# Attention scores on 64 rows: two softmax maps on the two row halves of the array

## Chip, cores, metric

The kernel runs on one core of one Trainium2 chip. The metric is the time of one execution in microseconds (us), the median of the runs.

## What is computed

A transformer block with one batch of 1024 tokens and 1024 channels, all in float32: a modulated layer norm, one input projection into queries, keys, values, a pooling branch and two gates, differential attention (8 heads, two softmax maps each), a gated sum with the pooled branch, an output projection, a norm, and a gated feed-forward layer with its norm. The part that matters here is the attention:

```python
def diff_attention(q, k, v, lam, slopes, sub_g, lambda_init):
    """q, k: (B,S,H,2,Dh); v: (B,S,H,Dv); lam: scalar. Returns (B,S,H*Dv)."""
    ...
        bias = -slopes[:, None, None] * dist[None]
        s = jnp.einsum('bqhmd,bkhmd->bhmqk', qblk, k,
                       preferred_element_type=jnp.float32) * scale + bias[None, :, None]
        p = jax.nn.softmax(s, axis=-1)
        a = p[:, :, 0] - lam * p[:, :, 1]
        return jnp.einsum('bhqk,bkhe->bqhe', a, v.astype(jnp.float32))
```

Here m counts the two maps, d the 64 channels of a map's queries and keys, and a block is 128 queries.

## The kernel before

Products run in the type float32r. To keep float32's accuracy, most operands x are split into xh (x rounded to float32r) and xl = x - xh, and a product a b is the sum of three: ah bh, ah bl and al bh (`mm3`, lines 98 to 101). Every TensorE instruction is a weight load of up to 128 x 128 and a product that streams up to 512 columns into one PSUM bank.

The program has a prelude (to 128 us: the first norm, the modulation, the pooling branch and the projections of head 0), the attention (some 128 to 860 us), the output projection and second norm, and the two layers of the feed-forward part. In the attention, the loop at line 808 runs over 8 heads and inside it, at line 855, over 8 blocks j of 128 queries. For one block, `scores` (line 619) forms the scores of both maps against all 1024 keys, a PSUM tile of 128 x 1024 for each (`ps_s`, two buffers in all, two banks each); VectorE adds the distance bias, takes the minimum for the softmax and moves the scores to SBUF (line 635); ScalarE takes the exponentials (line 637); VectorE takes the difference of the two maps (line 642). `transposes` (line 645) turns the result by 8 products with the identity, ScalarE and VectorE split it, and `av` (line 655) multiplies it with the values, 24 products of 256 columns for every second block. In a turn of j the scores of block j+1 are issued ahead of the transposes of block j. Beside that, `fill` (lines 814 to 837) spreads the projections of the next head and the gates over the turns: mostly 24 products of 512 columns for each.

A projection leaves the queries of a head as 128 rows x 512 tokens in PSUM, rows 0 to 63 for map 0 and rows 64 to 127 for map 1. Before, queries and keys are stacked. `evac_k` (line 497) puts kh of a map on its own 64 rows of a tile and kl of the same map on the other 64 rows, a tile for each map. `evac_q` (line 485) splits the queries of a map on its 64 rows into qh and ql, and a DMA copies both to the other 64 rows. A product on all 128 rows then gives qh kh + qh kl at once, and a second one ql kh + ql kl. So a map needs two products for each half of the keys (`kh` in the code counts these halves), and a block eight (lines 628 and 630), one map after the other.

Two parts of the program order their instructions by hand (`manual_schedule`): the prelude and what follows the attention. Within the attention a scheduler of the framework orders the instructions of each engine by priority (earlier in the program first) and by when it reckons that operands and buffers are ready; that order is fixed when the kernel is built. Each engine works through its own queue in order.

Of the kernel before, what the change touches and what calls it, by code (L numbers as in the profile page):

```python
# [9 lines left out]
F32 = mybir.dt.float32  # L10
F32R = mybir.dt.float32r
# [7 lines left out]
P = 128  # L19
# [16 lines left out]
def encoder_block_kernel(  # L36
# [22 lines left out]
    def ps_s(nm):  # L59
        return pp.tile([P, 1024], F32, tag="s", bufs=2, name=nm)  # L60
# [100 lines left out]
    # mod columns: GEMV of rows [128 k x 1024] accumulated on DVE, reduced over partitions by PE  # L161
# [40 lines left out]
    batch = [("u", 3, 3072 + 3 * P), ("u", 2, 3072 + 2 * P), ("q", 0, 0)]  # L202
    wb = {}
    with tc.tile_pool(name="pre", bufs=1, reuse_waits="tile") as pre:
# [99 lines left out]
        def batch_mm(g0, n0=0, n1=6, step=1):  # L304
            """The first products with the contraction outermost, as the tiles of h arrive."""
            if not pq:
                pq.extend((ps_g("pbq0"), ps_g("pbq1")))
            for k, (nm, g, _) in [(k, b) for k in (2 * g0, 2 * g0 + 1) for b in batch][n0:n1:step]:
                for hf in range(2):
                    cs = slice(hf * HF, (hf + 1) * HF)  # L310
                    ps = pq[hf] if nm == "q" else pb[nm, g][:, cs]
                    mm3(ps, wb[nm, g][0][:, k, :], wb[nm, g][1][:, k, :],
                        hT_h[:, k, cs], hT_l[:, k, cs], k == 0, k == KT - 1)
# [13 lines left out]
        def distances(i):  # L327
            """Half of the table of -|key - query|."""
            it = pre.tile([P, 960], I32, tag="hf", bufs=2, name="it%d" % i)
            tf = pre.tile([P, 960], F32, tag="hf", bufs=2, name="tf%d" % i)  # L330
            nc.gpsimd.iota(it, pattern=[[-1, 960]], base=896 - 960 * i, channel_multiplier=1)
            nc.gpsimd.tensor_copy(tf, it)
            return tf
# [77 lines left out]
        # lambda  # L411
# [69 lines left out]
    with ExitStack() as ctx2:  # L481
# [3 lines left out]
        def evac_q(h, hf, ps):  # L485
            sc = 2.0 ** (h - 2)
            for m in range(2):
                r = slice(m * DH, (m + 1) * DH)
                o = slice((1 - m) * DH, (2 - m) * DH)
                t = at1.tile([P, 2, HF], F32R, tag="qd%d" % m, bufs=3, name="q%d_%d_%d" % (h, hf, m))  # L490
                nc.scalar.mul(t[r, 0, :], ps[r, :], sc)
                nc.vector.scalar_tensor_tensor(t[r, 1, :], ps[r, :], sc, t[r, 0, :].bitcast(F32),
                                               op0=ALU.mult, op1=ALU.subtract)
                nc.sync.dma_start(t[o].bitcast(F32), t[r].bitcast(F32))
                qd[h, hf, m] = t

        def evac_k(h, hf, ps):
            cs = slice(hf * HF, (hf + 1) * HF)
            for m in range(2):
                if hf == 0:  # L500
                    kd[h, m] = at1.tile([P, S], F32R, tag="kd%d" % m, bufs=2, name="k%d_%d" % (h, m))
                t = kd[h, m]
                r = slice(m * DH, (m + 1) * DH)
                o = slice((1 - m) * DH, (2 - m) * DH)
                nc.scalar.copy(t[r, cs], ps[r, :])
                nc.vector.tensor_tensor(t[o, cs], ps[r, :], t[r, cs].bitcast(F32), op=ALU.subtract)
# [14 lines left out]
        # ---- pooling branch, with the projections of head 0  # L521
# [97 lines left out]
        def scores(h, j, zt):  # L619
            slope = 2.0 ** -(h + 1)  # L620
            hf, jj = divmod(j, 4)
            s = []
            for m in range(2):
                ps = ps_s("s%d_%d_%d" % (h, j, m))
                q = qd[h, hf, m]
                for kh in range(2):
                    cs = slice(kh * HF, (kh + 1) * HF)
                    nc.tensor.matmul(ps[:, cs], q[:, 0, jj * P:(jj + 1) * P], kd[h, m][:, cs],  # L628
                                     start=True, stop=False)
                    nc.tensor.matmul(ps[:, cs], q[:, 1, jj * P:(jj + 1) * P], kd[h, m][:, cs],  # L630
                                     start=False, stop=True)
                t = at.tile([P, S], F32, tag="s%d" % m, bufs=2, name="e%d_%d_%d" % (h, j, m))
                nm = small.tile([P, 1], F32, tag="nm", bufs=6, name="nm%d_%d_%d" % (h, j, m))
                o0 = 896 - P * j
                nc.vector.tensor_tensor_reduce(out=t, in0=ps, in1=table[:, o0:o0 + S], scale=-slope,  # L635
                                               scalar=3.0e38, op0=ALU.add, op1=ALU.min, accum_out=nm)
                nc.scalar.activation(t, t, AF.Exp, bias=nm, scale=-1.0, accum_out=zt[:, m, j:j + 1])  # L637
                s.append(t)
            c1 = small.tile([P, 1], F32, tag="c1", bufs=4, name="c1_%d_%d" % (h, j))
            nc.vector.reciprocal(c1, zt[:, 1, j:j + 1])  # L640
            nc.vector.tensor_scalar(c1, c1, nlam, zt[:, 0, j:j + 1], op0=ALU.mult, op1=ALU.mult)
            nc.vector.scalar_tensor_tensor(s[1], s[1], c1, s[0], op0=ALU.mult, op1=ALU.add)  # L642
            return s[1]
# [69 lines left out]
        # remaining modulation vectors  # L713
# [14 lines left out]
        # output projection; its first tiles run beside the last head  # L728
        ypart = {}

        def wo_scale(k):
            """w_out with its columns scaled by the gate g1, kept in DRAM until the last head."""
# [51 lines left out]
        def early_load(t):  # L784
            pool, tags, n = {0: (at1, ("kd0", "kd1"), 2), 1: (at1, ("qd0", "qd1"), 3), 4: (at1, ("vh", "vl"), 1),
# [171 lines left out]
    def rest_w(f, rawg, rawu, step):  # L957
        """Operands (gate, up columns) of the last five products of pair f: their sums and splits."""
# [183 lines left out]
    # Each pair of column tiles (gate, up) over both token halves is a 2x2 block product  # L1142
    # with seven block products (Winograd's form).
# [5 lines left out]
    def first_out():  # L1149
        """Operands of the first two steps of the second layer."""  # L1150
# [32 lines left out]
    # Token halves, halves of the hidden channels and column halves form 2x2 blocks again;  # L1183
    # the sums of blocks replace blocks that no later product reads.
    mA = big.tile([P, 16, HF], F32, tag="A", name="mA")
    mB = big.tile([P, 16, HF], F32, tag="B", name="mB")
    with tc.tile_pool(name="fo", bufs=1, reuse_waits="tile") as fo:
# [32 lines left out]
        def sums(q, k):  # L1220
            """Blocks, or sums of blocks, of the hidden activations and of the weights for two steps of product q."""
# [45 lines left out]
        def residual(z, c, cs, xr):  # L1267
            """z = alpha * x1 + g2 * c on the columns cs."""
# [3 lines left out]
        def shift(st):  # L1272
            """-mean * rstd, the bias of the norm on ScalarE."""
# [196 lines left out]
```

## Time and profile before

| | us |
|---|---|
| median of 3 runs | 1675.31 |
| lowest and highest run | 1674.59, 1677.12 |
| span of the profiled execution | 1677.4 |
| TensorE products busy in it | 1578.5 (94%) |
| VectorE busy | 1189.5 (71%) |
| ScalarE busy | 709.9 (42%) |
| GpSimd busy | 421.7 (25%) |
| score products, line 628 | 105.3 (256 products) |
| score products, line 630 | 101.5 (256 products) |

The profile is of one execution. Busy time is the union of the recorded instructions of an engine. Products on TensorE overlap (a record runs from the start of a product to its modelled end), so a group's busy time is more than the time for which it keeps the engine from other work; the starts tell that. PE stands for products and PEld for weight loads, DVE is VectorE, ACT ScalarE, POOL GpSimd, SP the engine that issues most DMAs.

### The profile page before, as it was taken

What the parts mean: (1) busy time and instruction counts of PE and PEld (TensorE: products, weight loads), DVE (VectorE), ACT (ScalarE), POOL (GpSimd) and SP (SyncE); (2) the same over time, 40 slices, a digit from 0 to 9 for tenths busy, and PEclk for the clock granted to TensorE, in tenths of its full rate; (3) what the DMA queues carried; (4) which work ended last, traced back from release to release, by engine and by line L of the source; (5) the groups of instructions that cost most, each with busy time, mean ns of one, the idle gap of its engine ahead of it and who ended that gap; (6) DMA issues with size and microseconds to landing.
All of it is one profiled execution on the core that took longest, in us unless ns stands there. A gap on an engine that the chain in (4) does not pass through costs nothing.

```text
span 1677.4 us, 20367 instructions
## 1 busy us (share of the span) xinstructions
PE 1578.5 (94%) x7634; PEld 1308.7 (78%) x7634; DVE 1189.5 (71%) x1664; ACT 709.9 (42%) x1228; POOL 421.7 (25%) x382
## 2 busy tenths in 40 slices
PE   5899999999999999999989979999999999969874
PEld 3787888888888888888878757888888888858653
DVE  7676868685966667675657896555555554898998
ACT  3445545454545545454532444333333334425341
POOL 4300001010102101000142471212111111574793
PEclk8999999999999999999999989999999999989997
DMA  9244334151433323213063513322322228724321
GB/s 332 60 122 145 105 95 132 45 150 64 133 94 101 120 82 119 57 57 101 27 224 131 170 51 100 97 80 78 99 76 86 77 89 290 255 76 150 107 107 63
DMA packets 169333, 190.76 MB, mean 114 GB/s; under 512 B 7185, under 2 KB 125010, under 8 KB 169234
## 3 DMA queue, kind: packets, MB, share of 16 engines
q1 hardware_dynamic: 165392, 176.06, 33.6%
q0 software_dynamic: 3184, 12.32, 2.0%
q8 instruction: 60, 0.98, 0.2%
q10 hardware_dynamic: 658, 1.08, 0.2%
q14 instruction: 39, 0.32, 0.1%
HBM read 144.34 MB, written 36.70 MB: 108 GB/s over the span
## 4 chain that ended last, share of the span: by engine, by line
PE 75%; DVE 14%; issue 4%; DMA 3%; POOL 3%; ACT 1%; SPq 0%; DVEq 0%; POOLq 0%; ACTq 0%
PE fa L99 4%; PE fa L100 4%; PE fa L101 4%; PE fb L99 3%; PE fb L100 3%; PE fb L101 3%; PE at L651 3%; PE s L628 3%; PE s L630 3%; DVE wo L96 2%; PE pp L99 2%; PE pp L100 2%; PE pp L101 2%; PE pv L99 2%; PE pv L100 2%
## 5 line engine op out<-in xcount | busy, mean ns | idle before, releaser
L637 ACT ACTIVATE e<-e,nm 128x1024 f32<-128x1024 f32 x128 | 147.1, 1150 | 111.1 <-DVE nm L635 109.8
L635 DVE CUSTOM_DVE_ANT_0 e<-s,table 128x1024 f32<-128x1024 f32 x128 | 153.1, 1217 | 24.9 <-PE s L630 24.4
L96 DVE TENSOR_TENSOR ol<-ws,oh 128x512 fp32r<-128x512 f32 x88 | 61.0, 695 | 76.4 <-ACT oh L95 76.3
L628 PE MATMUL s<-k,q 128*128 128x512 f32 x256 | 105.3, 411 | 1.2 <-DVE nm L635 1.2
L96 DVE TENSOR_TENSOR al<-at,ah 128x512 fp32r<-128x512 f32 x128 | 83.2, 684 | 31.9 <-ACT ah L95 31.4
L979 POOL TENSOR_TENSOR ws<-rg,ru 128x512 f32<-128x512 f32 x22 | 45.7, 2075 | 228.1 <-DVE ol L96 217.2
L630 PE MATMUL s<-k,q 128*128 128x512 f32 x256 | 101.5, 397 | 0.0
L95 ACT CAST oh<-ws 128x512 fp32r<-128x512 f32 x88 | 53.9, 616 | 104.4 <-POOL ws L979 66.7
L642 DVE SCALAR_TENSOR_TENSOR e<-e,c,e 128x1024 f32<-128x1024 f32 x64 | 87.4, 1365 | 1.9
L100 PE MATMUL oa<-wo,moh 128*128 128x512 f32 x176 | 73.0, 415 | 15.3 <-DVE wo L96 15.3
L95 ACT CAST ah<-at 128x512 fp32r<-128x512 f32 x128 | 70.0, 596 | 25.1 <-PE at L651 25.1
L99 PE MATMUL oa<-wo,moh 128*128 128x512 f32 x176 | 71.6, 407 | 3.3 <-ACT wo L95 3.3
L651 PE MATMUL at<-ident,e 128*128 128x128 f32 x512 | 68.9, 275 | 6.0 <-DVE e L642 3.2
L99 PE MATMUL av<-ah,vh 128*128 128x256 f32 x256 | 73.9, 289 | 0.3 <-ACT ah L95 0.2
L99 PE MATMUL fa<-oA,oh 128*128 128x512 f32 x176 | 69.8, 397 | 2.9 <-ACT oh L95 2.7
L101 PE MATMUL av<-ah,vl 128*128 128x256 f32 x256 | 72.6, 284 | 0.0
L100 PE MATMUL av<-al,vh 128*128 128x256 f32 x256 | 72.5, 283 | 0.0
L101 PE MATMUL oa<-wo,mol 128*128 128x512 f32 x176 | 71.9, 408 | 0.0
L101 PE MATMUL fa<-oA,ol 128*128 128x512 f32 x176 | 69.7, 396 | 1.1 <-DVE ol L96 1.0
L100 PE MATMUL fa<-oA,oh 128*128 128x512 f32 x176 | 69.6, 396 | 0.5 <-DVE oA L1051 0.5
L681 POOL TENSOR_TENSOR rm_1v<-rm_1s,rm_1v 128x4 f32<-128x4 f32 x8 | 5.0, 624 | 251.8 <-ACT rm_1s L672 251.8
L651 PEld LDWEIGHTS at<-ident,e 128*128 128x128 f32 x512 | 58.7, 144 | 11.7 <-DVE e L642 3.6
(562 smaller groups left out, 4812.3 us busy)
## 6 DMA issues: line engine op xcount, KB each, us to landing
ada<-in_w_ada_dram SPq DMA_DIRECT2D x32, 512.0 KB, 3.8
rg<-in_w_ffn_in_dram SPq DMA_DIRECT2D x26, 512.0 KB, 3.9
w<-in_w_ffn_out_dram SPq DMA_DIRECT2D x24, 512.0 KB, 3.9
ru<-in_w_ffn_in_dram SPq DMA_DIRECT2D x22, 512.0 KB, 3.8
midD<-th SPq DMA_DIRECT2D x42, 256.0 KB, 2.1
q<-q SPq DMA_DIRECT2D x32, 256.0 KB, 2.9
mt<-mixD SPq DMA_DIRECT2D x12, 448.0 KB, 6.4
x<-in_x_dram SPq DMA_DIRECT2D x8, 512.0 KB, 6.3
```

The costliest lines, as they stand in the source:

```text
L95: nc.scalar.copy(hi, src)
L96: (eng or nc.vector).tensor_tensor(lo, src, hi.bitcast(F32), op=ALU.subtract)
L99: nc.tensor.matmul(ps, lh, rh, start=start, stop=False, skip_group_check=skip)
L100: nc.tensor.matmul(ps, lh, rl, start=False, stop=False, skip_group_check=skip)
L101: nc.tensor.matmul(ps, ll, rh, start=False, stop=stop, skip_group_check=skip)
L628: nc.tensor.matmul(ps[:, cs], q[:, 0, jj * P:(jj + 1) * P], kd[h, m][:, cs], start=True, stop=False)
L630: nc.tensor.matmul(ps[:, cs], q[:, 1, jj * P:(jj + 1) * P], kd[h, m][:, cs], start=False, stop=True)
L635: nc.vector.tensor_tensor_reduce(out=t, in0=ps, in1=table[:, o0:o0 + S], scale=-slope, scalar=3.0e38, op0=ALU.add, op1=ALU.min, accum_out=nm)
L637: nc.scalar.activation(t, t, AF.Exp, bias=nm, scale=-1.0, accum_out=zt[:, m, j:j + 1])
L642: nc.vector.scalar_tensor_tensor(s[1], s[1], c1, s[0], op0=ALU.mult, op1=ALU.add)
L651: nc.tensor.matmul(pt[:, i, :], a[:, kt * P:(kt + 1) * P], ident, start=True, stop=True, is_transpose=True)
L979: pol(sa, r11, r21, op=ALU.subtract)
```

## The change

`evac_q` no longer makes a tile for each map and no DMA copies halves: one tile holds qh and ql of both maps on 128 rows, each map on the 64 rows on which the projection left it. `evac_k` likewise splits both maps at once into a tile of kh and one of kl. `scores` then issues, for each half of the keys, qh kh, qh kl and ql kh for each map, each product on 64 rows, in turns between map 0 (rows 0 to 63) and map 1 (rows 64 to 127): twelve products for a block. Both PSUM tiles are asked for at the start, and the softmax of both maps follows after all twelve products in the program. The small term ql kl is no longer computed. The query tiles have four buffers of one tag where there were three of each of two tags, and `early_load(1)`, which puts rows of the output projection into them, follows. All else in the diff is comments taken out.

```diff
         def evac_q(h, hf, ps):
             sc = 2.0 ** (h - 2)
-            for m in range(2):
-                r = slice(m * DH, (m + 1) * DH)
-                o = slice((1 - m) * DH, (2 - m) * DH)
-                t = at1.tile([P, 2, HF], F32R, tag="qd%d" % m, bufs=3, name="q%d_%d_%d" % (h, hf, m))
-                nc.scalar.mul(t[r, 0, :], ps[r, :], sc)
-                nc.vector.scalar_tensor_tensor(t[r, 1, :], ps[r, :], sc, t[r, 0, :].bitcast(F32),
-                                               op0=ALU.mult, op1=ALU.subtract)
-                nc.sync.dma_start(t[o].bitcast(F32), t[r].bitcast(F32))
-                qd[h, hf, m] = t
+            t = at1.tile([P, 2, HF], F32R, tag="qd", bufs=4, name="q%d_%d" % (h, hf))
+            nc.scalar.mul(t[:, 0, :], ps, sc)
+            nc.vector.scalar_tensor_tensor(t[:, 1, :], ps, sc, t[:, 0, :].bitcast(F32),
+                                           op0=ALU.mult, op1=ALU.subtract)
+            qd[h, hf] = t

         def evac_k(h, hf, ps):
             cs = slice(hf * HF, (hf + 1) * HF)
-            for m in range(2):
-                if hf == 0:
-                    kd[h, m] = at1.tile([P, S], F32R, tag="kd%d" % m, bufs=2, name="k%d_%d" % (h, m))
-                t = kd[h, m]
-                r = slice(m * DH, (m + 1) * DH)
-                o = slice((1 - m) * DH, (2 - m) * DH)
-                nc.scalar.copy(t[r, cs], ps[r, :])
-                nc.vector.tensor_tensor(t[o, cs], ps[r, :], t[r, cs].bitcast(F32), op=ALU.subtract)
+            if hf == 0:
+                kd[h] = [at1.tile([P, S], F32R, tag="kd%d" % i, bufs=2, name="k%d_%d" % (h, i)) for i in range(2)]
+            split(kd[h][0][:, cs], kd[h][1][:, cs], ps)
...
             s = []
+            pss = [ps_s("s%d_%d_%d" % (h, j, m)) for m in range(2)]
+            for kh in range(2):
+                cs = slice(kh * HF, (kh + 1) * HF)
+                for n_, (qi, ki) in enumerate(((0, 0), (0, 1), (1, 0))):
+                    for m in range(2):
+                        r = slice(m * DH, (m + 1) * DH)
+                        nc.tensor.matmul(pss[m][:, cs], qd[h, hf][r, qi, jj * P:(jj + 1) * P], kd[h][ki][r, cs],
+                                         start=n_ == 0, stop=n_ == 2)
             for m in range(2):
-                ps = ps_s("s%d_%d_%d" % (h, j, m))
-                q = qd[h, hf, m]
-                for kh in range(2):
-                    cs = slice(kh * HF, (kh + 1) * HF)
-                    nc.tensor.matmul(ps[:, cs], q[:, 0, jj * P:(jj + 1) * P], kd[h, m][:, cs],
-                                     start=True, stop=False)
-                    nc.tensor.matmul(ps[:, cs], q[:, 1, jj * P:(jj + 1) * P], kd[h, m][:, cs],
-                                     start=False, stop=True)
+                ps = pss[m]
...
-            pool, tags, n = {0: (at1, ("kd0", "kd1"), 2), 1: (at1, ("qd0", "qd1"), 3), 4: (at1, ("vh", "vl"), 1),
+            pool, tags, n = {0: (at1, ("kd0", "kd1"), 2), 1: (at1, ("qd", "qd"), 4), 4: (at1, ("vh", "vl"), 1),
```

## Rows read from the trace of the kernel before

**Rows 1.** Windows view, core 0: stretch, busy time (instructions) by engine, clock.

```profile
core 0: us, PE busy (x) PEld busy (x) DVE busy (x) ACT busy (x) POOL busy (x), PEclk, DMA share, GB/s
200.00:300.00 100.00, 99.59 (x550) 85.61 (x549) 74.24 (x114) 49.11 (x88) 8.03 (x20) 1.00 0.32 97
...
700.00:800.00 100.00, 99.69 (x537) 85.08 (x536) 68.98 (x111) 50.22 (x89) 6.29 (x18) 1.00 0.26 77
800.00:850.00 50.00, 48.80 (x288) 41.86 (x287) 33.79 (x58) 31.86 (x57) 18.37 (x21) 1.00 0.18 58
```

**Rows 2.** TensorE's waits, 128 to 870 us: sum, times, longest one.

```profile
PE at L651 <- DVE e L642: 3.2, 1, 3.2
...
PE at L651 <- DVE c L640: 1.6, 1, 1.6
PE s L628 <- DVE nm L635: 1.2, 5, 0.4
```

**Rows 3.** Timeline, one mid-head score block: start, duration, engine, line, operation.

```profile
290.63 0.49 PE L651 MATMUL at<-ident,e 128*128 128x128 f32 x3
...
290.85 0.19 PEld L628 LDWEIGHTS s<-k,q 128*128 128x128 f32 x1
290.88 0.47 PE L628 MATMUL s<-k,q 128*128 128x512 f32 x1
290.96 0.19 PEld L630 LDWEIGHTS s<-k,q 128*128 128x128 f32 x1
291.19 0.39 PE L630 MATMUL s<-k,q 128*128 128x512 f32 x1
291.19 0.19 PEld L628 LDWEIGHTS s<-k,q 128*128 128x128 f32 x1
...
292.81 0.40 PE L99 MATMUL pp<-hT_h,wp_h 128*128 128x512 f32 x1
```

**Rows 4.** Timeline: two score products after TensorE had waited.

```profile
609.14 0.50 PE L628 MATMUL s<-k,q 128*128 128x512 f32 x1 [0.15 <-DVE nm L635]
...
609.48 0.39 PE L630 MATMUL s<-k,q 128*128 128x512 f32 x1
```

**Rows 5.** Timeline of the prelude: three changes of the rows or columns used.

```profile
27.97 0.49 PE L249 MATMUL xtr<-ident,x 128*128 128x128 f32 x3
...
28.39 0.19 PEld L283 LDWEIGHTS psm<-ident,row 1*128 1x128 f32 x2 [0.17 <-issue]
...
39.89 0.28 PE L283 MATMUL psm<-ident,row 1*128 1x1 f32 x2 [0.45 <-ACT row L273]
40.09 0.30 PEld L286 LDWEIGHTS psm<-ones,ash 128*128 128x128 f32 x2
...
32.65 0.57 PE L286 MATMUL psm<-ones,ash 128*128 128x1 f32 x2
33.14 0.09 PEld L270 LDWEIGHTS gps<-rsc,cact 128*1 128x1 f32 x2
```

**Rows 6.** Windows view of score instructions: three cut-up stretches, one whole block (columns as rows 1).

```profile
316.50:318.00 1.50, 1.06 (x4) 0.75 (x4) 0.00 (x0) 1.00 0.00 0
323.50:325.50 2.00, 1.72 (x7) 1.31 (x7) 0.00 (x0) 1.00 0.01 4
328.00:328.45 0.45, 0.45 (x2) 0.20 (x2) 0.00 (x0) 1.00 0.79 273
...
347.80:350.50 2.70, 2.09 (x8) 1.43 (x8) 0.00 (x0) 1.00 0.44 126
```

**Rows 7.** Groups by line, queries' evacuation: busy, mean ns, idle before; its DMAs.

```profile
L492 DVE SCALAR_TENSOR_TENSOR q<-pq,q 64x512 fp32r<-64x512 f32 x28 | 19.2, 686 | 4.7 <-ACT q L491 4.3
...
L491 ACT ACTIVATE q<-pq 64x512 fp32r<-64x512 f32 x28 | 16.6, 593 | 27.2 <-DVE q L492 13.5 <-PE pq L101 12.2 <-PE s L630 1.5
...
q<-q SPq DMA_DIRECT2D x32, 256.0 KB, 2.9
```

## Prediction

> **What bounds the kernel now.** I read the stage windows first. From 200 to 800 us TensorE is busy for all but 0.2 to 0.4 us of every 100, at a granted clock of 1.00, that is 2.4 GHz, while VectorE is busy for 69 to 74 us of 100 and ScalarE for about 50 [rows 1]. Attention (128 to 850 us) is thus paced by TensorE: a microsecond taken from its products there shortens the kernel by about a microsecond, and work taken from VectorE or ScalarE gives nothing until a wait of TensorE hangs on it. The view of waits confirms that: of this whole stage TensorE's longest wait is 3.2 us, once, at its very end, for the softmax difference of line 642; then come 1.6 us once and 1.2 us in five pieces [rows 2].
>
> A busy TensorE is not one that streams at its rate, so I look at starts and not at durations. In one score block (query block j of head h) the first product starts 0.03 us behind the last transpose (three from 290.63, 0.11 apart), the second 0.31 us behind the first, and from there each follows the one before by 0.23 us, although a record lasts 0.39 us: from 291.19 to the next line's first product at 292.81 are seven products in 1.62 us, 0.23 each (0.228 over longer stretches) [rows 3]. The 0.39 us is latency, of which all but 0.23 is covered by the next product. In the same rows each weight load starts within 0.01 us of the start of the product ahead of it and lasts 0.19 us, so it is hidden, and two loads in a row start 0.11 us apart (290.85, 290.96). What an uncovered load costs is in the same block (0.31 instead of 0.23 to the second product) and where the engine had waited: 609.14 to 609.48, 0.34 us instead of 0.23 [rows 3, 4]. I take 0.11 us.
>
> **The terms.**
>
> *Products.* Before: 8 products of 512 columns for each of 64 blocks, 512 in all. After: 12, 768 in all, each on 64 rows. Were they to run one behind the other, they would cost 256 x 0.228 = 58.4 us more. Where a product on the lower and one on the upper rows run beside each other, 12 take the time of 6: 128 x 0.228 = 29.2 us less. No row of this trace shows two products side by side, so this term lies between -29.2 and +58.4. I take the overlap, because the two chains share nothing that I can see: other rows, other weights, and PSUM tiles of their own (the tiles of the two maps; each kh has its own accumulation within them). The Trainium skill, page "TensorE: Matmul & The Clock Gate", section "Measured speedup vs the span model", gives 3.07 times for four products on 32 rows with 512 columns. No run here shows that yet; by that page the term would be at its lower end.
>
> *Weights.* Twelve loads at 0.11 us are 1.32 us for a block against 6 x 0.228 = 1.37 us of streams: they just fit, with no slack. The upper half's chain cannot start until its own first load is done behind the first one, so it trails by one load, 0.11 us, in every stretch of score products.
>
> *Changes of shape.* This is what I find against the change. TensorE changes the shape of what it uses in a few places of the prelude, and in each the next weight load does not start beside the last product, as in rows 3, but only 0.07 to 0.08 us before that product's modelled end: the transposes of 27.97 end at 28.46 and the one-row load starts at 28.39, with 0.17 us of idle that no wait explains; the one-row products end at 40.17, the load of 128 rows starts at 40.09; products on 128 columns end at 33.22, the one-column load starts at 33.14 [rows 5]. Two more changes, at 19.92 and 24.24 us, show the same distance (five in all). So a new shape starts only when the array has all but run empty. The score products would bring a change from 128 rows to 64 and one back around every stretch. Going in from the transposes: their record lasts 0.27 us, so the load comes 0.20 us after the last one's start instead of at once: 0.20 us. Coming out: 0.39 - 0.07 = 0.32 us to the load, then 0.11 us of load that nothing hides, 0.43 instead of 0.23: 0.20 us. On 64 rows the latency may be shorter (a one-column product on 128 rows lasts 0.25 to 0.27 us, one on one row 0.19 to 0.22 [rows 5]), so I take 0.17. A stretch then costs 0.20 + 0.17 + 0.11 = 0.48 us; ends 0.45 and 0.51, and 0.11 if the 64 rows are no other shape at all. The Trainium skill, page "TensorEngine Tiling (Array Packing)", section "Key Properties", says that a change of tiling mode drains the engine while a change of tile within a mode does not; the trace agrees with the first half [rows 5], the second half is not shown here, and if it were false every one of the twelve products would pay.
>
> *How many stretches.* TensorE's order in this stage is the scheduler's. In the middle of a head the eight products of a block stand together (38 times), but at each change of head they are cut up to fill waits for the value transposes and for free PSUM: four, then seven, then two and three [rows 6]. In all the 512 products stand in 85 stretches. After, I see 64 to 100 and take 85, since the waits that cut them remain.
>
> *Evacuations.* For each of 16 halves of queries two ScalarE writes (0.593 us), two VectorE writes (0.686) and two DMAs (256 KB, 2.9 us to landing) become one, one and none; for keys two and two of about the same length become one and one [rows 7]. That is some 22 us less on VectorE, 19 us less on ScalarE and 32 issues less on SyncE's queue, all beside TensorE. What it can give back is bounded by TensorE's waits for such work, at most 2 us; I take nothing. The new tiles hold 8 KB less in each partition, which nothing waits for.
>
> *The added wait.* Both maps' products now alternate, so a block's second product needs both PSUM tiles free, and the first map's minimum (line 635, 1.2 us) can start only after the eleventh product, not the fourth. Queued behind it on TensorE is the block's remainder and the projections. In mid-head a block comes every 11 us and its result is needed a block later, so this costs nothing; at a change of head, where blocks stand some microseconds apart, and in the last head, where VectorE sets the pace, it may add up to 3 us each. I take zero and keep the 6 us for the range.
>
> **The sum.** 85 x 0.48 - 29.2 = +11.6 us. The profiled span of 1677.4 us is 2 us above the median of the runs and within their spread, so I add the difference to the median: 1675.3 + 11.6 = 1686.9 us. With 64 stretches at 0.45 it is -0.4 (1675), with 100 at 0.51 +21.8, and with the waits some +24 (1699): that is this case's own range.
>
> **The rivals.**
>
> *A, the halves overlap and 64 rows cost no drain (faster).* Then a stretch costs only the trailing load: 85 x 0.11 - 29.2 = -19.8 us, 1655; without any trailing 1646. It speaks for it that the gain of 29.2 us lies wholly on the engine that paces the stage. It decides from a price of 0.34 us for a stretch downwards (29.2 / 85). Against it: all five changes of shape in the trace drain.
>
> *B, no overlap (slower).* The halves take turns: +58.4 us, and 85 x 0.37 = 31 us of drains: +90 us, 1765. For it: no row of this trace shows two products at a time, and both halves' products write all 128 partitions of PSUM.
>
> *C, a half's next weights can't load beside its own stream.* Each product then takes 0.34 us as in rows 4, and six of them per half 0.11 x 6 = 0.68 us more for a block: +11.6 + 64 x 0.6 = +50 us, 1725. Against it: loads run beside streams on the same rows all through [rows 3]. The Trainium skill, page "TensorE: Matmul & The Clock Gate", section "The mechanism", says that loads overlap products in flight only where the row groups differ; rows 3 show otherwise for the full array, and by that page this rival would hold.
>
> *D, the scheduler parts the halves at the changes of head.* If one map's tile is free earlier, it may put six products of that map together and the other six later. Three of eight blocks per head, 24 in all, then run unpaired: 24 x 6 x 0.228 = 33 us more: 1720.
>
> **Chances.** Forecast 0.47, A 0.21, B 0.13, C 0.08, D 0.11. A change of under 0.2% (3.4 us) can hardly be told from none. Of the forecast's own range about 0.04 lies on the faster side of that, 0.13 within it and 0.30 above. So faster 0.25, same 0.13, slower 0.62. For 8 in 10 the range takes in the forecast, most of A, C and D, and leaves out B and A's far end: 1650 to 1727.
>
> **What would show it.** In the profile after: the starts of the score products. Overlap is right if two products on 64 rows start within 0.23 us; B if each starts 0.23 behind the last; C if same-half products stand 0.34 apart. The drain is right if the first score load starts 0.20 us behind the last transpose and the first projection's load 0.3 us behind the last score product; A if both start within 0.01. The stretches can be counted in the order of the products, and D shows as runs on one half alone. TensorE's waits for line 635 should stay under 6 us. The forecast fails most simply if the granted clock of 1.00 falls in this stage because half of the array rests; no row bears on that, so it has no term.

## The result, and the profile after

| | before | after |
|---|---|---|
| median of 4 runs, us | 1675.01 | 1713.07 |
| lowest and highest run, us | 1674.59, 1677.12 | 1712.01, 1714.21 |
| ratio, 95% interval | | 1.0225, 1.021 to 1.0239 |
| span of the profiled execution, us | 1677.4 | 1711.8 |
| VectorE, ScalarE busy, us | 1189.5, 709.9 | 1163.3, 686.7 |
| stretches of score products | 85 | 92 |

The change costs 38 us, where +11.6 was forecast. The page of after first: the span, TensorE's busy time and the 768 products of 64 rows (line 621; columns: line, engine, operation, operands, count, busy us and mean ns of one, idle before).

```profile
span 1711.8 us, 20712 instructions
...
PE 1614.8 (94%) x7890; PEld 1307.2 (76%) x7890; DVE 1163.3 (68%) x1632; ACT 686.7 (40%) x1196; POOL 422.2 (25%) x382
...
L621 PE MATMUL s<-k,q 64*128 64x512 f32 x768 | 136.0, 428 | 1.8 <-DVE nm L628 1.8
```

One product still lasts 0.43 us in the mean, but 768 of them are busy for 136 us, 0.18 each: they run two at a time. That was the hope behind the change, and it holds. The stage windows (columns as in [rows 1]) show what was not foreseen:

```profile
128.00:200.00 72.00, 70.58 (x370) 56.45 (x368) 48.68 (x72) 36.65 (x62) 1.46 (x3) 0.98 0.39 121
200.00:300.00 100.00, 99.53 (x540) 80.20 (x538) 67.28 (x102) 41.98 (x76) 6.72 (x18) 0.95 0.27 83
300.00:400.00 100.00, 99.54 (x537) 80.14 (x538) 68.03 (x103) 41.69 (x75) 6.68 (x18) 0.95 0.27 83
400.00:500.00 100.00, 99.53 (x525) 79.70 (x524) 66.12 (x101) 41.46 (x76) 6.63 (x18) 0.93 0.26 79
500.00:600.00 100.00, 99.47 (x574) 80.97 (x573) 61.16 (x96) 44.67 (x81) 16.34 (x22) 1.00 0.27 90
...
700.00:800.00 100.00, 99.53 (x569) 80.99 (x568) 62.90 (x100) 44.76 (x83) 7.92 (x24) 1.00 0.14 43
```

TensorE is as busy as before, and VectorE and ScalarE have more rest, so TensorE still paces the stage. But from 200 to 500 us its granted clock is 0.93 to 0.95 of 2.4 GHz, and 0.98 from 128 to 200; before it was 1.00 in all windows from 128 to 850 us ([rows 1] has three of them). Its waits (sum, times, longest) are no explanation:

```profile
PE vtr L508 <- ACT vT L505: 2.2, 8, 0.3
PE av L99 <- ACT ah L95: 1.9, 1, 1.9
PE s L621 <- DVE nm L628: 1.8, 2, 1.0
PE at L644 <- DVE vl L96: 1.5, 7, 0.4
```

Now a block in the middle of a head, where 12 products stand together (timeline; columns as in [rows 3]):

```profile
299.33 0.60 PE L644 MATMUL at<-ident,e 128*128 128x128 f32 x4
...
299.86 1.24 PEld L621 LDWEIGHTS s<-k,q 64*128 64x128 f32 x12 [0.17 <-issue]
299.86 1.67 PE L621 MATMUL s<-k,q 64*128 64x512 f32 x12
301.46 0.19 PEld L99 LDWEIGHTS pp<-hT_h,wp_h 128*128 128x128 f32 x1 [0.36 <-issue]
301.46 0.50 PE L99 MATMUL pp<-hT_h,wp_h 128*128 128x512 f32 x1
...
301.79 0.39 PE L100 MATMUL pp<-hT_l,wp_h 128*128 128x512 f32 x1
```

The last of the four transposes starts at 299.66; so the first score load comes 0.20 us behind it, after 0.17 us of idle that no wait explains. Two products of different halves then start 3 ns apart, the next two 0.34 us later (their loads are not hidden), and from there two every 0.23 us. The last starts at 301.145, the projection's load 0.31 us behind it, and the product after that another 0.33. From the last transpose to the second projection product it is 0.20 + 1.60 + 0.33 = 2.13 us; before it was 0.03 + 1.93 + 0.23 = 2.19 [rows 3]. Two fewer slots of 0.228 us are won in such a block, and all but 0.05 us or so of that is paid for the shape.

Where the 34.4 us between the two spans come in can be read from the start of the value projection's first product at each change of head:

| value projection for head | 1 | 2 | 3 | 4 | 5 | 6 | 7 |
|---|---|---|---|---|---|---|---|
| after minus before, us | 1.5 | 8.8 | 16.4 | 25.4 | 28.2 | 30.2 | 32.2 |

Inside a head nothing is lost or won: in the middle of head 2 the products pp, at 386 us before, stand at +16.3, and the value projection for head 3, at that head's end, at +16.4. Each change of head costs 2.0 to 2.8 us, and the first three 7.2, 7.7 and 9.0. One of these three, in the timeline and in windows, with the change from head 3 to 4 as the last window:

```profile
235.26 0.85 PE L177 MATMUL adaps<-ones,acc 128*128 128x1 f32 x6
...
235.98 1.10 PE L644 MATMUL at<-ident,e 128*128 128x128 f32 x4
237.00 2.21 PEld L621 LDWEIGHTS s<-k,q 64*128 64x128 f32 x6 [0.33 <-issue]
237.00 2.93 PE L621 MATMUL s<-k,q 64*128 64x512 f32 x6
...
239.86 1.11 PE L644 MATMUL at<-ident,e 128*128 128x128 f32 x4
...
240.90 2.93 PE L621 MATMUL s<-k,q 64*128 64x512 f32 x6
```

```profile
230.00:235.50 5.50, 5.23 (x33) 3.75 (x31) 2.89 (x4) 1.53 (x2) 0.00 (x0) 1.00 0.12 22
235.50:246.50 11.00, 11.00 (x33) 7.71 (x33) 6.30 (x13) 5.82 (x10) 0.00 (x0) 0.53 0.10 36
...
535.00:546.00 11.00, 10.73 (x59) 7.69 (x58) 7.28 (x13) 6.00 (x10) 0.00 (x0) 1.00 0.17 49
```

Two things are seen. The block is parted: six products of map 0, four transposes, six products of map 1, each six alone on its half, 0.43 us apart. And the clock stands at its lower level, 1.2 GHz, from 236 to 246 us: in these 11 us TensorE has 33 products, in the last window 59. What TensorE did before the clock fell: four value transposes, one 64-row product, and 16 one-column products (line 177, the sums of a modulation column, 234.1 to 236.0). The four transposes behind them already start 0.21 us apart, where those at 299 us start 0.11 apart.

### The profile page after: what moved, and what is told of

Its sections match the earlier page's. It is cut to its first block, busy times and chain, and to the rows that moved or that the text cites. A ratio compares the mean times of both kernels' runs of the same rounds, so it can differ in the third digit from the quotient of the medians.

```text
span 1711.8 us, 20712 instructions
## 1 busy us (share of the span) xinstructions
PE 1614.8 (94%) x7890; PEld 1307.2 (76%) x7890; DVE 1163.3 (68%) x1632; ACT 686.7 (40%) x1196; POOL 422.2 (25%) x382
## 3 DMA queue, kind: packets, MB, share of 16 engines
q8 instruction: 62, 1.02, 0.2%
## 4 chain that ended last, share of the span: by engine, by line
PE 76%; DVE 11%; issue 4%; POOL 4%; DMA 3%; ACT 2%; SPq 0%; DVEq 0%; POOLq 0%; ACTq 0%
PE s L621 6%; PE fa L101 4%; PE fa L100 4%; PE fa L99 4%; PE at L644 3%; PE fb L99 3%; PE fb L101 3%; PE fb L100 3%; DVE wo L96 2%; PE pp L99 2%; PE pk L99 2%; PE pa L99 2%; PE pq L99 2%; PE pp L100 2%; PE pp L101 2%
## 5 line engine op out<-in xcount | busy, mean ns | idle before, releaser
L621 PE MATMUL s<-k,q 64*128 64x512 f32 x768 | 136.0, 428 | 1.8 <-DVE nm L628 1.8
L621 PEld LDWEIGHTS s<-k,q 64*128 64x128 f32 x768 | 81.5, 192 | 34.9 <-issue 18.2
L635 DVE SCALAR_TENSOR_TENSOR e<-e,c,e 128x1024 f32<-128x1024 f32 x64 | 83.3, 1301 | 2.0
L644 PE MATMUL at<-ident,e 128*128 128x128 f32 x512 | 72.6, 283 | 1.9 <-DVE vl L96 1.5
```

Of the source, the lines that this page charges most:

```text
L621: nc.tensor.matmul(pss[m][:, cs], qd[h, hf][r, qi, jj * P:(jj + 1) * P], kd[h][ki][r, cs], start=n_ == 0, stop=n_ == 2)
L644: nc.tensor.matmul(pt[:, i, :], a[:, kt * P:(kt + 1) * P], ident, start=True, stop=True, is_transpose=True)
```

## The experiments

Theory 1 was then: the shape costs about as much as it saves, and the loss comes from the clock, which falls where one-column sums and half-array products meet at a change of head. Each experiment was timed beside the kernel before on its own chip; its median there (1674.2 to 1676.7) is the measure.

**The sums moved away.** Only the place of the 16 one-column products differs from the changed kernel: they go to the fourth block of the next head (for which the accumulator has a second buffer).

```diff
                     if kk == KT - 1:
-                        ada_fin(jj)
+                        fins.append(jj)
...
+                if fins and j == 3:
+                    ada_fin(fins.pop())
```

> The changed kernel, with the column sums of the modulation (16 one-column products at four changes of head) moved to block 3 of the next head. Theory 1: the granted clock falls at the first three changes of head because these sums, which stream one column each, stand together there with score products on one half of the rows; away from them the clock stays at 1.00. The three changes of head then cost as little as the later ones (some 2.3 us each and not 7 to 9): 17 us less, about 1696 us. Theory 2: the products on one half of the rows, six in a row, bring the clock down alone: it falls as before, about 1713 us.

Measured: 1693.07 us, ratio 1.0096 (1.0078 to 1.0113), 20.0 us less than after. The windows, and the block that follows the transposes at the change from head 4 to 5, with the minimum that VectorE takes meanwhile:

```profile
200.00:300.00 100.00, 99.53 (x566) 81.26 (x563) 71.11 (x108) 44.37 (x80) 7.08 (x18) 1.00 0.29 90
300.00:400.00 100.00, 99.53 (x578) 81.66 (x578) 71.09 (x109) 45.27 (x83) 8.60 (x23) 1.00 0.28 86
400.00:500.00 100.00, 99.53 (x566) 81.15 (x565) 70.13 (x107) 45.03 (x81) 7.75 (x23) 1.00 0.25 80
```

```profile
617.56 1.09 PE L644 MATMUL at<-ident,e 128*128 128x128 f32 x8
618.33 1.22 DVE L628 CUSTOM_DVE_ANT_0 e<-s,table 128x1024 f32<-128x1024 f32 x1
618.58 2.25 PEld L621 LDWEIGHTS s<-k,q 64*128 64x128 f32 x12 [0.17 <-DVE nm L628]
618.58 2.68 PE L621 MATMUL s<-k,q 64*128 64x512 f32 x12
621.19 0.50 PE L99 MATMUL pq<-hT_h,wq_h 128*128 128x512 f32 x1
```

The clock is back at 1.00 in these windows and with it 20 us; the mean granted clock of its four runs is 0.974 to 0.977, that of after's four 0.964 and 0.965. Every change of head now costs 1.9 to 2.2 us. The price of the sums' neighbourhood is settled.

One fall is left that the sums have no part in: from 153.7 to 157 us here, and at the same place in after, where the window shows it:

```profile
154.00:157.50 3.50, 3.11 (x12) 2.65 (x12) 3.05 (x6) 1.17 (x2) 0.00 (x0) 0.52 0.65 181
```

Ahead of it stand two blocks of 64-row products, with 0.75 us of waiting between them, and no one-column product in the 50 us before.

The remaining 17 us are not settled: the block at the change of head still takes 2.61 us from its first product to the projection, against 1.60 in the middle of a head. Its order is six of one map and then six of the other, and only four of the twelve run beside another. But it is not the order that delays the second map: its first load and product start at 619.61 us, 0.06 us behind the end of the minimum (618.33 + 1.22 = 619.55) that gives back the PSUM tile they need. The kernel that holds the order and moves the sums, further down, shows the same 2.6 us.

**The alternation kept.** The changed kernel, the twelve products held in the order of the program.

```diff
+                        mm = nc.tensor.matmul(pss[m][:, cs], qd[h, hf][r, qi, jj * P:(jj + 1) * P],
+                                              kd[h][ki][r, cs], start=n_ == 0, stop=n_ == 2)
+                        if mms:
+                            tc.add_manual_dep(mm.ins, mms[-1].ins.name, mybir.DependencyInfo(
+                                mybir.DependencyClass.NoSync, mybir.DependencyReason.DATA), reason="order")
+                        mms.append(mm)
```

> The changed kernel, with each block's twelve score products tied to their order in the program, so that the scheduler can't put six of one map together at a change of head; stretches are still cut up (93). Theory 1 (serial halves are one cost, the clock another, set off by the column sums): the six serial pairs of a block are gained back at each change of head, 1.4 us times 8, 11 us, and the clock still falls: about 1702 us. Theory 2 (the serial halves bring the clock down): the clock stays at 1.00 too, some 17 us more: about 1685 us. If serial halves cost nothing: 1713 us.

Measured: 1706.54 us, 1.0175 (1.0153 to 1.0197), 6.5 us less than after. From 200 to 500 us the clock falls less (0.98, 1.00 and 0.98 in the three windows); from 500 to 600 it is 0.97, where after had 1.00. Yet a change of head still costs 2.0 us and more. So the fall does not need the parted halves, though in sum it is shorter without them, and holding the order has a price: TensorE's waits for a free PSUM tile (line 628, here 633) go from 1.8 to 7.1 us.

**No alternation.** The other way round: in every block six products of map 0, then six of map 1.

```diff
-            for kh in range(2):
-                cs = slice(kh * HF, (kh + 1) * HF)
-                for n_, (qi, ki) in enumerate(((0, 0), (0, 1), (1, 0))):
-                    for m in range(2):
-                        r = slice(m * DH, (m + 1) * DH)
+            for m in range(2):
+                r = slice(m * DH, (m + 1) * DH)
+                for kh in range(2):
+                    cs = slice(kh * HF, (kh + 1) * HF)
+                    for n_, (qi, ki) in enumerate(((0, 0), (0, 1), (1, 0))):
```

> The changed kernel, with all six products of map 0 ahead of the six of map 1 in every block. If the two halves overlap only when products on them alternate, a whole block takes 12 and not 6 times 0.23 us: 1.37 us more for some 54 blocks, 74 us, and about 1787 us, more where the clock falls. If alternation does not matter, 1713 us.

Measured: 1741.30 us, 1.0386 (1.0362 to 1.041), between the two theories. A mid-head block:

```profile
268.06 2.23 PE L621 MATMUL s<-k,q 64*128 64x512 f32 x12
270.21 0.50 PE L99 MATMUL pk<-hT_h,wk_h 128*128 128x512 f32 x1
```

It takes 2.16 us instead of 1.60; 0.56 us in the 38 whole blocks that alternated in after are 21 of the 28 us by which this kernel is slower. In strict order it would take 2.74 us (12 x 0.228). The twelve starts are two chains: 268.06, 268.39, 268.62, 268.86, 269.09, 269.32 and 268.63, 268.96, 269.20, 269.43, 269.67, 269.89. So map 1's first product starts 6 ns behind map 0's third, ahead of three that precede it in the program and, as the kernel is built, in TensorE's queue. The two chains' assignment to the maps is read from their spacing: no product of one half follows another of it in under 0.22 us.

**One shape change by itself.** The kernel before, with one product more in each of its 64 blocks, overwritten by the next: in one kernel on 128 rows, in the other on 64.

```diff
+                    if m == 0 and kh == 0:
+                        nc.tensor.matmul(ps[:, cs], q[0:64, 0, jj * P:(jj + 1) * P],
+                                         kd[h, m][0:64, cs], start=True, stop=True)
                     nc.tensor.matmul(ps[:, cs], q[:, 0, jj * P:(jj + 1) * P], kd[h, m][:, cs],
```

> The kernel before, with one product more in each of the 64 blocks of scores: on 128 rows, at the head of map 0's first pair, its sum overwritten by the next product. Both theories: 64 x 0.228 us = 14.6 us more than before, so 1690; it is the measure for the kernel beside it. Granted clock as before (0.98).

> The same extra product on 64 rows instead of 128, so each block has one change of shape in and one out, and nothing else of the change. Theory 1, the shape changes cost what the forecast put on them (0.17 to 0.34 us for in and out together beyond the product itself): 11 to 22 us above the kernel with the extra 128-row product, 1701 to 1712, granted clock as before. Theory 2, in and out are hidden behind the weight loads and the stretches cost nothing: the same time as with 128 rows, 1690. Theory 3, a 64-row product near the sums of the modulation columns is enough to bring the clock down: 15 us more still, with the granted clock at 0.95 or less in 200 to 500 us.

Measured: 1689.55 us (1.0087, 1.0062 to 1.0112) with 128 rows, 15.3 us above before where 14.6 were expected, and 1715.34 us (1.0236, 1.0214 to 1.0258) with 64, on one chip. 25.8 us / 64 = 0.40 us for going into the shape and out of it. One such block of the second kernel (lines 631 and 633 are the products of before):

```profile
507.32 0.18 PEld L629 LDWEIGHTS s<-k,q 64*128 64x128 f32 x1 [0.16 <-issue]
507.32 0.50 PE L629 MATMUL s<-k,q 64*128 64x512 f32 x1
507.75 0.19 PEld L631 LDWEIGHTS s<-k,q 128*128 128x128 f32 x1 [0.24 <-issue]
507.75 0.50 PE L631 MATMUL s<-k,q 128*128 128x512 f32 x1
507.86 0.19 PEld L633 LDWEIGHTS s<-k,q 128*128 128x128 f32 x1
508.09 0.40 PE L633 MATMUL s<-k,q 128*128 128x512 f32 x1
```

In 0.20 us behind the last transpose, 0.43 to the next product and 0.34 to the one after: 0.97 us. With full rows the three are 0.03, 0.31 and 0.23 [rows 3]: 0.57. The difference is the same 0.40. Some of the 25.8 us is clock, though. In windows of 100 us the granted clock stayed at 0.98 or above, so theory 3 falls as it was put (0.95 or less, 15 us more). But behind three of the four sums it stood at its lower level for three to four us (0.51 from 239.0 to 242.5, from 338.0 to 341.5 and from 536.0 to 539.5), and in the kernel with 128 rows behind one of them:

```profile
234.00:238.00 4.00, 4.00 (x15) 3.24 (x14) 2.72 (x5) 2.32 (x4) 0.00 (x0) 0.57 0.39 114
```

By the starts of the value projections from head 1 on, the kernel with 64 rows loses 3.0 to 3.1 us to the one with 128 over eight blocks where the clock did the same in both, that is 0.37 to 0.39 for each, and 4.5 over the two stretches where it alone had a fall. So the shape costs 0.37 to 0.40 us; below, 0.40 is used. And sums beside products on 128 rows can bring the clock down too.

**Both edits, and a whole block at the change of head.** First the two edits together; then also the next head's first block issued ahead of the value projections, which puts it in one piece; then this with the sums moved but the order left to the scheduler; and the same early issue in the kernel before.

```diff
-                for fn in fill[j]:
-                    fn()
                 if j == 7 and not last:
                     zt = small.tile([P, 2, 8], F32, tag="zt", bufs=2, name="zt%d" % n)
                     nxt_a = scores(n, 0, zt)
+                for fn in fill[j]:
+                    fn()
```

> The changed kernel with both edits tried one by one: the sums of the modulation columns moved away from the change of head, and the twelve products held in the order of the program. Theory 1, what they save adds up (20.0 and 6.5 us, the latter because no six products of one half run alone): 1713.1 - 26.5 = 1686.6. Theory 2, holding the order saved only by keeping the clock up, which the moved sums already do: 1693 (1691 to 1697).

> As the kernel before it in this list, and the next head's first block of scores issued ahead of the value projections at a change of head, so that this block stands whole instead of in pieces of 4, 4 and 4. Theory 1, each piece more costs 0.3 to 0.5 us: up to 7 x 2 x 0.45 = 6 us less than the kernel with two edits. Theory 2, the pieces fill waits at the change of head: no gain or a loss of some us.

> The changed kernel with the sums moved away and the next head's first block of scores issued ahead of the value projections, so that it stands whole; the order inside the twelve left to the scheduler. Theory 1, holding the alternation is worth as much as it costs in waits, and a whole block at the change of head is worth what it was in the kernel with all three edits (5.1 us): 1693.1 - 5 = 1688. Theory 2, the scheduler parts the halves of the next block instead, and nothing is won: 1693.

> The kernel before with only the issue of the next head's first block moved ahead of the value projections; its stretches of score products fall from 85 to 80. Theory 1, a cut costs much only where it changes the array's shape: within 2 us of before, 1672 to 1676. Theory 2, the gain of the whole block is a matter of the order and not of the shape: 5 us less, 1669.

| kernel | median, us | ratio | 95% interval |
|---|---|---|---|
| sums moved | 1693.07 | 1.0096 | 1.0078 to 1.0113 |
| sums moved, order held | 1696.71 | 1.0124 | 1.0105 to 1.0144 |
| all three | 1691.61 | 1.0097 | 1.0074 to 1.0120 |
| sums moved, early block | 1689.11 | 1.0081 | 1.0063 to 1.0099 |
| before, early block | 1688.72 | 1.0075 | 1.0058 to 1.0092 |

The savings do not add: with the clock at 1.00 from 200 us on already, holding the order gives nothing. The block at the change of head takes 2.6 us as it did with the sums alone moved, now with a wait in it:

```profile
621.57 0.50 PE L622 MATMUL s<-k,q 64*128 64x512 f32 x1
622.60 1.66 PE L622 MATMUL s<-k,q 64*128 64x512 f32 x11 [0.53 <-DVE nm L633]
```

Its second product needs the other map's PSUM tile, which comes free 1.0 us after the first. Where the scheduler lets six products of one map run in that time, nothing is lost by it; so the block's extra 1.0 us is the price of needing both tiles at once, not of the parted halves. The early block gives 5.1 us where the order is held (runs of 1690.3 to 1692.8 against 1694.5 to 1697.2 us on one chip); without that, the intervals overlap and no gain is shown. In the kernel before, the early block costs 12.0 us, against both theories. TensorE's wait for a free PSUM tile there, 1.2 us in [rows 2], is now

```profile
PE s L628 <- DVE nm L635: 8.3, 9, 1.1
```

which is 7 of the 12 us. The clock fell there as well, from 523 to 526 us behind the sums, with all score products on 128 rows (0.98 from 500 to 600 us); the rest is open. So the pieces at a change of head are not waste: they stand where TensorE would wait.

**Whole blocks everywhere.** The order held, the twelve given priority over other products, and a block's first product kept until the previous block's second minimum is done, so that nearly all stand whole (63 of 67 stretches).

```diff
...
+                            if not mms and last_min[0] is not None:
+                                tc.add_manual_dep(mm.ins, last_min[0].ins.name, mybir.DependencyInfo(
+                                    mybir.DependencyClass.Sync, mybir.DependencyReason.DATA), reason="both free")
```

> The changed kernel, with the twelve products of a block in their order, given priority over other products, and held back until both PSUM tiles are free: 67 stretches and not 92, 63 of them whole blocks. If cutting the blocks up (with the serial halves and the fall of the clock that go with it) is the whole loss, what stays is a block of 0.20 + 6 x 0.23 + 0.20 us in place of 8 x 0.228: 0.05 us less for each of 64, so about 1672 us, 3 us under the kernel before. If the clock falls at the column sums whatever the score products do: about 1689 us. If something else of the change costs time (the new query and key tiles, the later softmax of map 0), it stays near 1713 us.

Measured: 1754.81 us, 1.0468 (1.0442 to 1.0494). Fewer stretches, and slower than all others and than any of the three expectations. TensorE's waits:

```profile
PE vtr L508 <- ACT vT L505: 25.0, 16, 2.9
PE s L625 <- DVE nm L639: 20.7, 22, 1.3
PE at L655 <- DVE vl L96: 6.3, 7, 1.3
PE at L655 <- ACT e L641: 5.4, 1, 5.4
```

57 us of waits against 7.4 in the rows of after. The blocks take 1.60 us as in after, and the clock is low for about as long (0.95 to 0.98 in the windows from 128 to 700 us); what the cuts had covered lies open.

**The sums, brought back elsewhere.** The kernel with the sums moved, and 16 such one-column products on a constant at the changes 4 to 5, 5 to 6 and 6 to 7, which have no weight columns' transfers beside them.

```diff
+                if 4 <= h <= 6 and j == 7:
+                    px = ps_av("adapx%d" % h)
+                    for k in range(KT):
+                        nc.tensor.matmul(px[:, k:k + 1], ident, ones[:, 0:1], start=True, stop=True)
```

> The kernel with the sums of the modulation columns moved away (1693.1), and at the three changes of head 4 to 5, 5 to 6 and 6 to 7 the same one-column products on a constant, their sums read by nobody: three changes of head that had none in any kernel so far, and without the weight columns' transfers and VectorE's sums that go on in heads 0 to 3. Their own time is 3 x 1.7 us. Theory 1, one-column products among 64-row products bring the clock down: granted clock under 1.00 after some of these changes (at 615, 708 and 800 us), 5 to 6 us each, 1704 to 1716. Theory 2, it is something else in heads 0 to 3 (the transfers, VectorE's sums): 1698, granted clock 1.00 from 500 to 850.

Measured: 1702.06 us, 1.0155 (1.0139 to 1.0171), 9.9 us more by the ratios than without, 5.1 of them the copies' own by the estimate above. Windows at the three places:

```profile
615.00:625.00 10.00, 9.73 (x53) 7.58 (x52) 6.16 (x11) 4.92 (x9) 0.00 (x0) 0.83 0.18 52
...
710.00:720.00 10.00, 9.73 (x60) 7.35 (x59) 5.95 (x10) 5.32 (x9) 0.00 (x0) 1.00 0.19 54
...
805.00:815.00 10.00, 9.73 (x49) 7.76 (x49) 4.20 (x6) 4.08 (x6) 0.00 (x0) 0.75 0.33 97
815.00:825.00 10.00, 10.00 (x40) 7.76 (x37) 6.14 (x11) 3.26 (x7) 0.00 (x0) 0.73 0.00 0
```

The clock falls at two of the three, where it stood at 1.00 from 500 to 850 us with the sums moved and no copies. The time is just under what theory 1 allowed, since the fall was short at the first and absent at the second. So such products beside the score products are enough, without the transfers or VectorE's sums of the early heads. Why one change of three is spared here, and that of head 3 to 4 in after, with the same sequence, stays open. Nor do falls come at the same places in every execution: the one at 154 us is absent here, though up to there the kernel is the one with the sums moved. Each kernel has one trace.

## Why the forecast was wrong

The direction, the overlap and the price of the shape were right; two terms that the forecast put at nothing were not, the clock (some 17 to 20 us) and the wait for both PSUM tiles (some 7). 1686.9 us were forecast, 1713.1 came, inside the range and on none of its cases. That rival D's 1720 lies nearest is chance: its mechanism costs 7 us and not 33.

- **Products, -29.2 us: right.** Two halves run side by side, 0.23 us for two. Rivals B and C fall: no product waits for the other half, and loads run beside their own half's stream, 12 in 1.24 us.
- **The trailing load, 0.11 us a stretch: wrong.** The halves start 3 ns apart. But two loads are then open and the second pair comes 0.34 us behind the first, much as the second product of a block did before (0.31) [rows 3].
- **The drain: right.** Forecast 0.20 in and 0.17 out, and 0.48 with the trailing load; measured 0.37 to 0.40 for the whole. In was 0.20 to the digit; out the load came 0.31 to 0.32 us behind the last product, and not earlier for the half's shorter path. Rival A falls. The Trainium skill, page "TensorEngine Tiling (Array Packing)", section "Key Properties", says that a change of mode drains the engine and that different tiles work in parallel; the two rows of idle before a load, 0.16 and 0.24 us, and the pairs 3 ns apart agree with both.
- **Stretches: 92, not 85,** within the range. 92 x 0.40 - 29.2 = +7.6 us stands where +11.6 stood. These steps taken alone were 4 us too high, so they are not why the forecast failed.
- **Rival D: it came, and smaller.** It was held to be another case than the forecast, when it is a part of it. At the changes of head the scheduler parts the halves, but in one block of three, and even so four of twelve may overlap: 1.0 us each, not 33 us in all. Nor is the parting the cost: with the order held the block takes the same 2.6 us. With these 1.0 us a change of head can be summed. In the kernel with the sums moved, at head 4 to 5, the three blocks take 8.73 us in six stretches (each from the start of the product ahead of it to that of the product behind it), before 6.74 in five. By terms: six slots fewer, -1.37; six shapes at 0.40, +2.40; the block that waits for its second tile, +1.02; together +2.05, measured +2.0.
- **The clock: the term that was missing.** The sum takes the clock of 1.00 as given, because "no row bears on that, so it has no term", and this was the largest of all: 20.0 us by the moved sums, 17 us by the first three changes (7.2 + 7.7 + 9.0 less 3 x 2.2). The risk was named, though for the wrong reason: half an array at rest in mid-head costs nothing (1.00 from 500 to 800 us); between 200 and 850 us the falls of 10 to 14 us came only with the one-column sums beside it, in after at three of the four changes of head that have them. Those sums stand in the trace of before at 232, 326, 419 and 513 us, at a clock of 1.00; that they neighbour the score products of a change of head could have been read there, and a price put on a clock at half for some microseconds.
- **The added wait, put at zero: wrong.** As idle time of TensorE it is right, 1.8 us in two waits for line 628, under the 6 us allowed. But a block that needs both PSUM tiles takes 1.0 us longer at each of the seven changes of head, some 7 us, whether the engine waits or runs one map alone meanwhile. Where the order is held it shows as waits: 7.1 us, and 9.2 with the sums moved.
- **The evacuations: right.** VectorE has 26 us less to do, ScalarE 23, and the kernel has nothing from it.
- **Readings that were off, without weight here:** from 200 to 800 us VectorE was busy for 64 to 75 us of 100 before, not 69 to 74, and TensorE idle for 0.1 to 0.4; 21.8 us and the 6 for waits make 27.8, not 24, at the upper end of the forecast's own range; and the span of 1677.4 us lies above the highest run, not within the spread.

For the queries, the two groups of [rows 7] are now

```profile
L490 DVE SCALAR_TENSOR_TENSOR q<-pq,q 128x512 fp32r<-128x512 f32 x14 | 9.6, 688 | 16.0 <-ACT q L489 16.0
...
L489 ACT ACTIVATE q<-pq 128x512 fp32r<-128x512 f32 x14 | 8.3, 594 | 26.5 <-PE pq L101 26.5
```

half as many, on all 128 partitions at the same length, and the queries' DMAs are gone.

Together, by the starts up to the last head: 1.5 us in the first head, where the clock fell at 154 us, 17 us of clock at the first three changes, and seven changes of head at 2.0 to 2.8 us (about 16; the whole blocks between two changes, at -0.05 each, are already in it). That makes 34.5, and the spans differ by 34.4. The medians differ by 38.1. In all other runs the time is 1.7 to 2.0 us above the span, so the profiled execution of before took some 1679.3 us, 4 us above its median, and that of after 0.6 above its own. Where in its trace the execution of before lost these 4 us is not known.

## What to carry to other kernels

A product on part of the rows is to be priced by the stretch, not by the product: here 0.40 us for each stretch against 0.46 us saved in a block, so the gain in the middle of a head is 0.05 us, and each cut turns it into a loss. Before splitting the array, count in the trace of before how many stretches the order has, see which of the cuts cover waits (taking five out cost 12 us in the kernel before, taking 25 out 42 us in the one after), and look which other thin products stand beside them. And two halves share all their time only if the order alternates (1.60 us for a block against 2.16) and the buffers of both are free: where one comes free 1.0 us after the other, the block took 2.6 us in either order.

## What the hardware showed that was not expected

- TensorE's clock fell to 1.2 GHz (236 to 246 us) while the engine had little idle time (5.23 us busy of the 5.50 before, 11.00 of the 11 from there on), at three of four changes of head where 16 one-column products stood near 64-row ones. With the sums moved it stayed at 1.00 from 200 to 850 us. Neither is needed, though: behind the same sums beside 128-row products it was 1.00 in the kernel before, but fell at one of four places in the kernel with the extra 128-row product (0.57 from 234 to 238 us) and at one of four in the kernel before with the early block (523 to 526 us); and it fell at 154 us behind 64-row products without sums (0.52). These falls were shorter, three to four us against 10 to 14. What decides whether one comes stays open.
- Products on different halves start out of the program's order: one began 6 ns behind the third of six that stood ahead of it. So the sentence ahead of the prediction, that each engine works through its queue in order, does not hold for TensorE between halves. The Trainium skill, page "TensorE: Matmul & The Clock Gate", section "The mechanism", says that products start and end strictly in program order; the starts in the kernel without alternation differ, so the measurement decides.
